# Gate pairs two to eight: the turning moved to VectorE, h added by accumulating loads, the finish of a pair moved behind the next pair

## The chip, the cores and the metric

The kernel runs on one core of one Trainium2 chip. Its time is the device time in microseconds of one execution. The five engines that the text speaks of are TensorE (PE; its weight loads are listed apart as PEld), VectorE (DVE), ScalarE (ACT), GpSimd (POOL) and SyncE (SP). SP issues most transfers; POOL issues the stores of the result.

## The reference

The reference is one inference step of a trunk with one layer, for T = 2080 rows (2048 of a prompt, 32 of a running stream) of width 1024, in float32. What matters here is the last of its three steps. With `h` the state after the mixers, `p` an input of 256 channels a row, and `g_final` a vector:

```
h   = h + concat(mixer_A, mixer_B) @ W_out
e   = p @ W_ple                                    # (T,256) @ (256,1024)
h   = h + e * sigmoid(rmsnorm(h) @ W_gate)         # (T,1024) @ (1024,1024)
out = rmsnorm(h) * g_final
```

The gate's product `rmsnorm(h) @ W_gate` has to be taken of the transposed rows, since TensorE contracts over partitions. The norm's factor is a number for each row; it is applied as the `scale` of the sigmoid.

## The kernel before

The 2080 rows are 16 tiles of 128 rows and a short one of 32. Every float32 operand of a product is split in two float32r parts: ACT copies it (L77, the high part), DVE subtracts that copy (L78, the low part), and three products (high·high, high·low, low·high) are added up in PSUM.

Products with square weights go by pairs of tiles: `seven` computes a pair's (256 x 1024) @ (1024 x 1024) product with seven half-size products in place of eight, each 12 matmuls of 128x128 by 128x512 (L167). The seven left operands are `11`, `12`, `22` and the sums `S1` to `S4`; the right ones are quarters of the weight and sums of them (`wg_a` to `wg_d`, `wg_T` and so on). A product lands in a PSUM bank (`x_g`, `y_g`, `z_g`), is carried (ACT copy) or is an output. `seven` takes a dictionary of steps to be recorded after its products, 1 to 6. A scheduler then orders the instructions of each engine; `tc.keep_in_program_order` pins one to its recorded place.

The stages of the program: input projection and mixers to about 560 us; the product with `W_out` by pairs to about 726 us; the embedding `e` in blocks (L102) to about 762 us, which writes `e` to DRAM, and meanwhile the gate's weights are loaded (`wg_r`, three buffers of the ring `xh`), split and added up on ACT and DVE; the short tile's gate (`gl`); eight gate pairs `g0` to `g14`, of about 20 us each; the last of them is `last_pair`, which computes the second tile's `e` itself (weights `wl`).

In a gate pair, while the products of pair `i` run, `prep_g(i + 2)` makes the left operands of the next one. The pair's second tile is loaded as four blocks (128 KB each) and turned by one DVE instruction (`turned_here`, STREAM_TRANSPOSE, L1293). The first tile is loaded as it is (`hn`, 512 KB), copied by ACT in two halves (`ho`, L1280) and turned by eight PE transposes into PSUM (`pth`, L1282). DVE makes the sums (L1426), and ACT and DVE split the results (L77, L78).

The outputs (`gate_ops`): ACT copies a bank (L1302), DVE adds a further product (L1310), ACT takes the sigmoid (L1308, L1311), DVE multiplies it into `e` (L1313) and adds that to `h` (L1314), for four halves a pair. `h` and `e` are loaded by SP. After the pair, for each of its tiles (`done_g`): squares on ACT (L88), mean and power on POOL (L69, L73), one DVE scaling by the root and `g_final` (SCALAR_TENSOR_TENSOR, L1321), and a store issued by POOL (L1322).

The buffers in question: `xh` has three (before: raw weights, then `h`), `ya` five (`hn`, `e`), `qa` two (`ho`), PSUM six banks for products and two for transposes.

Of the kernel before, what the change touches and what calls it, by code (L numbers as in the profile page):

```python
# [12 lines left out]
ALU = mybir.AluOpType  # L13
PSUM = bass.MemoryType.PSUM

P = 128
# [10 lines left out]
NT = SEQ // P + 1  # L27
NH = D // 2
# [6 lines left out]
def trunk(ctx, tc, x_p, x_s, c_conv, c_pool, p_p, p_s, g_mix, w_in, conv_w, conv_b, pool_w,  # L35
          pool_scale, w_out, g_ple, w_gate, w_ple, g_fin, y_p, y_s, sc_p, sp_p, sc_s, sp_s):
    nc = tc.nc
# [6 lines left out]
    h_d = tc.dram_tile([T, D], F32, name="h_d")  # L44
# [262 lines left out]
    def ring4(t, name):  # L307
        return t.tile([P, D], F32, tag="t", name=name)
# [15 lines left out]
    def load_rows(pool, name, i, pr, sa=None):  # L324
        r, n = tiles[i]
        t = ring4(pool, f"{name}_{i}")
        nc.sync.dma_start(t[:n], pr[r:r + n] if sa is None else rows_of(pr, sa, r, n))
        return t

    with ExitStack() as s1:  # L330
# [17 lines left out]
        def put(piece, src):  # L348

            split(piece[:, :, 0], piece[:, :, 1], src)  # L350
# [750 lines left out]
    with ExitStack() as s2:  # L1101
# [13 lines left out]
        def half_of(x, at, n=P):  # L1115
            return x[at[0]][:n, at[1] * NH:at[1] * NH + NH]
# [155 lines left out]
        def turned(i):  # L1272

            r, n = tiles[i]
            t = load_rows(ya, "hn", i, h_d).rearrange("p (q k c) -> p k q c", q=4, k=KC)
            out = []
            for half in range(2):
                pt = tbank(f"pth_{i}_{half}")
                o = qa.tile([P, KH, P], F32, tag="q", name=f"ho_{i}_{half}")
                nc.scalar.copy(o[:n].rearrange("p k (q c) -> p k q c", q=4), t[:n, half * KH:half * KH + KH])  # L1280
                for k in range(KH):
                    nc.tensor.transpose(pt[:, k * P:k * P + n], o[:n, k], ident[:n, :n])  # L1282
                out.append(pt.rearrange("p (k t) -> p k t", k=KH))
            return out

        def turned_here(i):

            r, n = tiles[i]
            t = ring4(ya, f"hn_{i}")
            for q in range(4):  # L1290
                nc.sync.dma_start(t[q * 32:q * 32 + 32].rearrange("p (g c) -> p g c", g=4),
                                  h_d[r:r + P, q * 256:q * 256 + 256].rearrange("(g p) c -> p g c", p=32))
            nc.vector.transpose(t, t)  # L1293
            u = t.rearrange("p (g k t) -> p k g t", g=4, k=KC)
            return u[:, :KH], u[:, KH:]

        def gate_ops(h, e, n, name, i):
            scale = lambda at: rs_h[:n, i + at[0]:i + at[0] + 1]

            def carry(ps, at):  # L1300
                t = st.tile([P, NH], F32, tag="t", name=f"c_{name}_{at[0]}{at[1]}")
                nc.scalar.copy(t[:n], ps[:n])  # L1302
                return t

            def out(ps, c, at):
                if c is None:
                    c = st.tile([P, NH], F32, tag="t", name=f"g_{name}_{at[0]}{at[1]}")
                    nc.scalar.activation(c[:n], ps[:n], AF.Sigmoid, scale=scale(at))  # L1308
                else:
                    nc.vector.tensor_tensor(c[:n], ps[:n], c[:n], op=ALU.add)  # L1310
                    nc.scalar.activation(c[:n], c[:n], AF.Sigmoid, scale=scale(at))  # L1311
                ee, hh = half_of(e, at, n), half_of(h, at, n)
                nc.vector.tensor_tensor(ee, ee, c[:n], op=ALU.mult)  # L1313
                nc.vector.tensor_tensor(hh, hh, ee, op=ALU.add)  # L1314

            return carry, out

        def done_g(i, h):
            r, n = tiles[i]
            rf = sumsq(h, n, f"f{i}")  # L1320
            nc.vector.scalar_tensor_tensor(h[:n], h[:n], rf[:n], g_bc[:n], op0=ALU.mult, op1=ALU.mult)  # L1321
            nc.gpsimd.dma_start(rows_of(y_p, y_s, r, n), h[:n])  # L1322

        def short_ops(h, e, n):
# [17 lines left out]
        def last_pair(i, A):  # L1342
# [72 lines left out]
        def prep_g(i):  # L1415

            A = {}
            whole = lambda t: t.rearrange("p k (g t) -> p k g t", g=4)

            def put(q, src, view=lambda t: t):  # L1420
                A[q] = cmb.tile([P, KH, 2, P], F32R, tag="c", name=f"g{i}_{q}")
                split(view(A[q][:, :, 0]), view(A[q][:, :, 1]), src)

            def comb(q, x, y, op, view=lambda t: t):
                t = ss.tile([P, KH, P], F32, tag="s", name=f"g{i}_f{q}")
                nc.vector.tensor_tensor(view(t), x, y, op=op)  # L1426
                return t

            lower = []

            def first():
                lower.extend(turned_here(i + 1))

            def second():
                a21, a22 = lower
                s1 = comb("S1", a21, a22, ALU.add, whole)
                a11, a12 = turned(i)
                put("11", a11)
                s2 = comb("S2", s1, a11, ALU.subtract)
                s3 = comb("S3", whole(a11), a21, ALU.subtract, whole)  # L1440
                put("12", a12)
                put("S2", s2)
                s4 = comb("S4", a12, s2, ALU.subtract)
# [17 lines left out]
        done_g(NT - 1, h)  # L1461
# [37 lines left out]
```

## Time and profile before

| | |
|---|---|
| median of three runs | 942.25 us (947.01, 942.25, 941.83) |
| profiled execution | 942.12 us, of which the span is 940.3 us |
| mean granted clock of TensorE | 0.994 |
| gate pairs two to seven | 19.93 to 20.15 us each |
| bytes moved | 127.23 MB read, 54.86 MB written |

The profile's page gives the busy time of each engine as a share of the span, the chain of work that ended last (followed back from the last instruction), groups of instructions with mean duration and what ended the idle time before them, and the transfers with their time to landing. Busy time of an engine beside the one that sets the end costs nothing.

### The profile page before, as it was taken

Reading aid. Unit: us, or ns where it says so; the run is one execution under the profiler, and the core shown is the slowest. Engines: PE = TensorE matmul, PEld = TensorE weight load, DVE = VectorE, ACT = ScalarE, POOL = GpSimd, SP = SyncE. Lnnn points to the kernel's source line nnn. Section 1 sums busy time; section 2 is a strip of 40 time slices with the busy share of each in tenths; the row PEclk is TensorE's granted clock in tenths of the full one; section 3 lists DMA queues with packets and bytes.
Section 4 is the critical chain, followed back from the end, with each engine's and each line's share of the span. In section 5 each row is a group of like instructions: output and inputs, shape, how many; then the busy total and the mean of one; then the engine's idle time right before and its main releaser. Section 6 shows DMA issues by size and latency. Waiting matters only on the chain.

```text
span 940.3 us, 13055 instructions
## 1 busy us (share of the span) xinstructions
PE 920.7 (98%) x4599; PEld 831.5 (88%) x4599; DVE 726.3 (77%) x1230; ACT 480.5 (51%) x890; POOL 126.2 (13%) x244
## 2 busy tenths in 40 slices
PE   7999999999999999999999999999999999999996
PEld 5999999999999999999999987888878868888885
DVE  6697998899587978785777588765554797888985
ACT  5554555454444554443454356334334875555564
POOL 2101222120000110000000010211211001211113
PEclk8999999999999999999999999999999999999999
DMA  8336586696952655418655359865785883566653
GB/s 247 101 105 172 143 243 197 182 255 207 423 166 80 178 161 144 151 52 287 198 167 176 117 176 305 263 194 170 217 253 171 307 274 130 201 227 209 216 207 112
DMA packets 133214, 182.96 MB, mean 195 GB/s; under 512 B 11164, under 2 KB 105116, under 8 KB 131869
## 3 DMA queue, kind: packets, MB, share of 16 engines
q1 hardware_dynamic: 117165, 131.70, 45.2%
q0 software_dynamic: 13248, 44.93, 14.9%
q10 hardware_dynamic: 2736, 5.51, 1.8%
q8 instruction: 36, 0.59, 0.3%
q14 instruction: 29, 0.24, 0.1%
HBM read 127.23 MB, written 54.86 MB: 194 GB/s over the span
## 4 chain that ended last, share of the span: by engine, by line
PE 74%; DMA 3%; DVE 2%; ACT 2%; issue 0%; POOL 0%; POOLq 0%; DVEq 0%; ACTq 0%
PE x_o L167 9%; PE x_g L167 9%; PE e L102 5%; PE z_g L167 5%; PE x_zab L556 5%; PE z_o L167 4%; PE x_ch L556 4%; PE x_zbv L556 4%; PE z_zab L556 2%; PE y_g L167 2%; PE y_o L167 2%; PE b L556 2%; PE v L556 2%; PE zb L556 2%; PE za L556 2%; PE c L556 2%
## 5 line engine op out<-in xcount | busy, mean ns | idle before, releaser
L77 ACT CAST y_S<-y_fS 128x512 fp32r<-128x512 f32 x32 | 19.5, 621 | 42.5 <-PE x_o L167 18.9
L102 PE MATMUL e<-wq,pps 128*128 128x512 f32 (+1 forms) x156 | 38.8, 399 | 0.2 <-ACT pps L77 0.2
L406 DVE SCALAR_TENSOR_TENSOR xt<-xt,rstd_x,g_bc 128x1024 f32<-128x1024 f32 (+2 forms) x18 | 23.1, 1282 | 19.4 <-POOL rstd_x L73 18.0
L167 PE MATMUL x_g<-wg_b,g_S 128*128 128x512 f32 x128 | 35.9, 390 | 0.0
L167 PE MATMUL x_o<-wo_b,y_S 128*128 128x512 f32 x128 | 35.8, 391 | 0.0
L556 PE MATMUL z_ch<-B,w_ch_S 128*128 128x416 f32 x168 | 34.3, 352 | 0.9 <-ACT U L851 0.9
L556 PE MATMUL z_zab<-B,w_zab_S 128*128 128x416 f32 x168 | 34.1, 351 | 0.5 <-ACT U L851 0.5
L556 PE MATMUL x_zab<-B,w_zab_S 128*128 128x416 f32 x168 | 34.5, 352 | 0.1
L556 PE MATMUL z_zbv<-B,w_zbv_S 128*128 128x416 f32 x168 | 34.2, 352 | 0.0
L556 PE MATMUL x_zbv<-B,w_zbv_S 128*128 128x416 f32 x168 | 34.1, 351 | 0.0
L556 PE MATMUL x_ch<-B,w_ch_S 128*128 128x416 f32 x168 | 34.0, 351 | 0.0
L102 PEld LDWEIGHTS e<-wq,pps 128*128 128x128 f32 (+1 forms) x156 | 27.4, 182 | 6.9 <-ACT pps L77 0.5
L556 PEld LDWEIGHTS z_ch<-B,w_ch_S 128*128 128x128 f32 x168 | 31.2, 188 | 1.6 <-ACT U L851 1.2
L556 PEld LDWEIGHTS z_zab<-B,w_zab_S 128*128 128x128 f32 x168 | 31.3, 188 | 1.1 <-ACT U L851 0.8
L556 PEld LDWEIGHTS x_zab<-B,w_zab_S 128*128 128x128 f32 x168 | 31.2, 188 | 1.0 <-DVE w_zab_S L78 0.4
L556 PEld LDWEIGHTS x_ch<-B,w_ch_S 128*128 128x128 f32 x168 | 31.4, 188 | 0.3
L556 PEld LDWEIGHTS x_zbv<-B,w_zbv_S 128*128 128x128 f32 x168 | 31.3, 188 | 0.3
L556 PEld LDWEIGHTS z_zbv<-B,w_zbv_S 128*128 128x128 f32 x168 | 31.3, 188 | 0.4
L69 POOL TENSOR_SCALAR ms_f<-ssq_f 128x1 f32<-128x1 f32 (+1 forms) x15 | 8.8, 585 | 160.7 <-ACT junk L88 160.7
L77 ACT CAST y<-y 128x512 fp32r<-128x512 f32 x24 | 14.8, 618 | 29.4 <-PE x_o L167 13.8
L1321 DVE SCALAR_TENSOR_TENSOR h<-h,rstd_f,g_bc 128x1024 f32<-128x1024 f32 (+1 forms) x15 | 19.3, 1284 | 12.7 <-POOL rstd_f L73 12.7
L167 PEld LDWEIGHTS x_o<-wo_b,y_S 128*128 128x128 f32 x128 | 24.0, 188 | 5.0 <-ACT c_o L1125 0.3
(570 smaller groups left out, 2670.7 us busy)
## 6 DMA issues: line engine op xcount, KB each, us to landing
y<-y_d SPq DMA_DIRECT2D x16, 512.0 KB, 12.7
x<-in_x_prompt_dram SPq DMA_DIRECT2D x16, 512.0 KB, 9.7
h_d<-x SPq DMA_DIRECT2D x16, 512.0 KB, 4.5
h<-h_d SPq DMA_DIRECT2D x16, 512.0 KB, 3.6
xt<-in_x_prompt_dram SPq DMA_DIRECT2D x15, 512.0 KB, 12.7
e<-e_d SPq DMA_DIRECT2D x15, 512.0 KB, 5.9
out_dram<-h POOLq DMA_DIRECT2D x14, 512.0 KB, 3.0
p_dT<-T POOLq DMA_DIRECT2D x12, 512.0 KB, 6.2
```

The source lines that it names most:

```text
L69: nc.gpsimd.tensor_scalar(ms[:n], ssq[:n], scalar1=1.0 / D, scalar2=EPS, op0=ALU.mult, op1=ALU.add)
L77: ins = nc.scalar.copy(hi, src)
L102: nc.tensor.matmul(ps[:n], pps[:, a, k, :n], wp[k][b][:, cs], start=k + q == 0, stop=k == 1 and q == 2)
L167: nc.tensor.matmul(ps[:n], lhs[:, k, a, :n], w[b][:, k], start=start and k + q == 0, stop=k == KH - 1 and q == 2, skip_group_check=True)
L406: nc.vector.scalar_tensor_tensor(xt[:n], xt[:n], r[:n], g_bc[:n], op0=ALU.mult, op1=ALU.mult)
L556: nc.tensor.matmul(ps[:, :NB], lhs[:, k, x], b[:, k, y], start=start and k + q == 0, stop=stop and k == KH - 1 and q == 2, skip_group_chec ...
L1321: nc.vector.scalar_tensor_tensor(h[:n], h[:n], rf[:n], g_bc[:n], op0=ALU.mult, op1=ALU.mult)
```

## The change

Four edits, all in the gate's pairs:

- `prep_g` has an argument `here`. For pairs two to eight (`here=True`) both tiles are loaded as four blocks each, at the start of the pair before, into the ring `xh`, and both are turned by DVE. For the first pair (`here=False`) the first tile is still turned by PE. All views of the operands are the blocks' (`whole`).
- `gate_ops` with `h is None` (all pairs but the last): the DVE addition of `h` goes; an accumulating load of the half tile of `h`, issued by POOL, adds it to the product of `e` and the sigmoid in place. The pair's tiles of `h` are not loaded any more, and the result stands in the buffer of `e`.
- `done_g` is cut in two, `root_g` (squares, mean, power) and `done_g` (scaling, store), both recorded in the next pair, at its steps 4 and 6; in `last_pair` at 4 and, behind the second half's last product, at 5.
- The scaling is pinned in program order (`keep_in_program_order`), and so are the squares (`later=True` of `sumsq`).

```diff
-        def turned_here(i):
+        def blocks(i):
             r, n = tiles[i]
-            t = ring4(ya, f"hn_{i}")
+            t = ring4(xh, f"hn_{i}")
             for q in range(4):
                 nc.sync.dma_start(t[q * 32:q * 32 + 32].rearrange("p (g c) -> p g c", g=4),
                                   h_d[r:r + P, q * 256:q * 256 + 256].rearrange("(g p) c -> p g c", p=32))
+            return t
+
+        def turned_here(t):
             nc.vector.transpose(t, t)
...
-                ee, hh = half_of(e, at, n), half_of(h, at, n)
+                ee = half_of(e, at, n)
                 nc.vector.tensor_tensor(ee, ee, c[:n], op=ALU.mult)
-                nc.vector.tensor_tensor(hh, hh, ee, op=ALU.add)
+                if h is None:
+                    r = tiles[i + at[0]][0]
+                    nc.gpsimd.dma_start(ee, h_d[r:r + P, at[1] * NH:at[1] * NH + NH], accum_op=ALU.add)
+                else:
+                    hh = half_of(h, at, n)
+                    nc.vector.tensor_tensor(hh, hh, ee, op=ALU.add)
...
-        def done_g(i, h):
+        def root_g(i, h, later=True):
+            return sumsq(h, tiles[i][1], f"f{i}", later=later)
+
+        def done_g(i, h, rf, later=True):
             r, n = tiles[i]
-            rf = sumsq(h, n, f"f{i}")
-            nc.vector.scalar_tensor_tensor(h[:n], h[:n], rf[:n], g_bc[:n], op0=ALU.mult, op1=ALU.mult)
+            ins = nc.vector.scalar_tensor_tensor(h[:n], h[:n], rf[:n], g_bc[:n], op0=ALU.mult, op1=ALU.mult)
+            if later:
+                tc.keep_in_program_order(ins)
             nc.gpsimd.dma_start(rows_of(y_p, y_s, r, n), h[:n])
...
-            seven(f"g{i}", A, W, carry, out, {5: lambda: second(1, NH)}, first_tile=True)
+            seven(f"g{i}", A, W, carry, out, {4: roots, 5: lambda: (second(1, NH), finished())}, first_tile=True)
...
-            lower = []
+            rows = [blocks(i + b) for b in range(1 - here, 2)]
+            ready = []
             def first():
-                lower.extend(turned_here(i + 1))
+                ready.extend(turned_here(rows[0]))
             def second():
-                a21, a22 = lower
-                s1 = comb("S1", a21, a22, ALU.add, whole)
-                a11, a12 = turned(i)
-                put("11", a11)
-                s2 = comb("S2", s1, a11, ALU.subtract)
+                if here:
+                    a11, a12 = ready
+                    put("11", a11, whole)
+                    a21, a22 = turned_here(rows[1])
+                    s1 = comb("S1", a21, a22, ALU.add, whole)
+                else:
+                    a21, a22 = ready
+                    s1 = comb("S1", a21, a22, ALU.add, whole)
+                    a11, a12 = map(whole, turned(i))
+                    put("11", a11, whole)
+                s2 = comb("S2", whole(s1), a11, ALU.subtract, whole)
...
-        for step in prep_g(0).values():
+        for step in prep_g(0, here=False).values():
...
+        def roots():
+            for x in ready:
+                x.append(root_g(*x))
+        def finished():
+            while ready:
+                done_g(*ready.pop(0))
         for i in range(0, NT - 3, 2):
             A = S.pop(i)
-            h = [load_rows(xh, "h", i + b, h_d) for b in range(2)]
+            steps = prep_g(i + 2)
             e = [load_rows(ya, "e", i + b, e_d) for b in range(2)]
-            seven(f"g{i}", A, W, *gate_ops(h, e, P, f"g{i}", i), prep_g(i + 2))
-            for b in range(2):
-                done_g(i + b, h[b])
+            seven(f"g{i}", A, W, *gate_ops(None, e, P, f"g{i}", i), {**steps, 4: roots, 6: finished})
+            ready.extend([i + b, e[b]] for b in range(2))
```

More of the change, by code (lines that the diff above doesn't have):

```diff
@@ L1411, in last_pair, with prep_g @@
             pps = embedded()
-            seven(f"g{i}", A, W, carry, out, {5: lambda: second(1, NH)}, first_tile=True)
+            seven(f"g{i}", A, W, carry, out, {4: roots, 5: lambda: (second(1, NH), finished())}, first_tile=True)
             second(0, NH // 2)
-        def prep_g(i):
+        def prep_g(i, here=True):
             A = {}
@@ L1427, in comb @@
                 return t
-            lower = []
+            rows = [blocks(i + b) for b in range(1 - here, 2)]
+            ready = []
             def first():
-                lower.extend(turned_here(i + 1))
+                ready.extend(turned_here(rows[0]))
             def second():
-                a21, a22 = lower
-                s1 = comb("S1", a21, a22, ALU.add, whole)
-                a11, a12 = turned(i)
-                put("11", a11)
-                s2 = comb("S2", s1, a11, ALU.subtract)
-                s3 = comb("S3", whole(a11), a21, ALU.subtract, whole)
-                put("12", a12)
+                if here:
[9 more added lines that the diff above has]
+                s2 = comb("S2", whole(s1), a11, ALU.subtract, whole)
+                s3 = comb("S3", a11, a21, ALU.subtract, whole)
+                put("12", a12, whole)
                 put("S2", s2)
-                s4 = comb("S4", a12, s2, ALU.subtract)
+                s4 = comb("S4", a12, whole(s2), ALU.subtract, whole)
                 put("S1", s1)
@@ L1460, in trunk @@
         plain("gl", A, W, n, *short_ops(h, e, n))
-        done_g(NT - 1, h)
+        done_g(NT - 1, h, root_g(NT - 1, h, False), False)
+        ready = []
+        def roots():
[4 more added lines that the diff above has]
+                done_g(*ready.pop(0))
         for i in range(0, NT - 3, 2):
             A = S.pop(i)
-            h = [load_rows(xh, "h", i + b, h_d) for b in range(2)]
+            steps = prep_g(i + 2)
             e = [load_rows(ya, "e", i + b, e_d) for b in range(2)]
-            seven(f"g{i}", A, W, *gate_ops(h, e, P, f"g{i}", i), prep_g(i + 2))
-            for b in range(2):
-                done_g(i + b, h[b])
+            seven(f"g{i}", A, W, *gate_ops(None, e, P, f"g{i}", i), {**steps, 4: roots, 6: finished})
+            ready.extend([i + b, e[b]] for b in range(2))
         last_pair(NT - 3, S[NT - 3])
```

## The prediction

> **What bounds the kernel now.** I read the page first: the shares of the engines, then the chain that ended last.
>
> ```profile
> PE 920.7 (98%) x4599; PEld 831.5 (88%) x4599; DVE 726.3 (77%) x1230; ACT 480.5 (51%) x890; POOL 126.2 (13%) x244
> PE 74%; DMA 3%; DVE 2%; ACT 2%; issue 0%; POOL 0%; POOLq 0%; DVEq 0%; ACTq 0%
> ```
>
> TensorE (PE) is busy 98% of the span and carries the chain; nothing else has more than 3% of it. The change concerns the last fifth, so next comes the table by windows there, one row per gate pair (columns: length, then PE, PEld, DVE, ACT and POOL busy, granted clock, share of the DMA engines, GB/s).
>
> ```profile
> 787.80:807.75 19.95, 19.95 (x93) 16.57 (x93) 17.65 (x27) 11.70 (x21) 3.49 (x6) 1.00 0.43 143
> 827.73:847.67 19.94, 19.94 (x94) 16.60 (x93) 17.43 (x27) 11.39 (x20) 3.36 (x6) 1.00 0.63 216
> 887.54:907.69 20.15, 20.15 (x95) 16.76 (x95) 17.67 (x27) 11.49 (x21) 3.36 (x6) 1.00 0.66 236
> 907.69:940.30 32.61, 24.61 (x109) 19.82 (x107) 22.30 (x36) 16.40 (x31) 10.40 (x16) 0.95 0.33 119
> ```
>
> A pair is 19.94 us of PE without a gap at full clock, so within a pair only PE work counts, as long as the others keep inside it. VectorE (DVE) is close behind with 17.4. Only in the last window is PE idle, for 32.61 − 24.61 = 8.0 us. The chain, read by start and duration, shows what PE does in a pair:
>
> ```profile
> 785.78 0.87 PE pth L1282 x8
> 786.65 1.15 PE z_g L167 x5
> 787.80 5.44 PE x_g L167 x24
> 793.24 2.72 PE y_g L167 x12
> 805.26 0.44 PE pth L1282 x4
> 805.93 0.44 PE pth L1282 x4
> ```
>
> Seven products of 12 matmuls at 2.72 are 19.04; the eight transposes (pth) are the other 0.87 to 0.88.
>
> **1. The transposes.** Pairs two to eight lose theirs: 56 of them, 7 × 0.88 = 6.2 us, all on the path.
>
> ```profile
> L1282 PE MATMUL pth<-ident,ho 128*128 128x128 f32 x56 | 7.4, 272 | 0.0
> L1280 ACT COPY ho<-hn 128x512 f32<-128x512 f32 x12 | 6.8, 622 | 0.0
> L1293 DVE STREAM_TRANSPOSE hn<-hn 128x1024 f32<-128x1024 f32 x6 | 7.4, 1237 | 0.0
> L1314 DVE TENSOR_TENSOR h<-h,e 128x512 f32<-128x512 f32 x24 | 15.9, 685 | 0.2
> ```
>
> The 7.4 counts overlapping ends, so it is the upper bound; I take 6.2, the chain's figure. In their place comes, per pair, one more STREAM_TRANSPOSE (1.24 on DVE), four adds of h go (4 × 0.685 = 2.74), and ScalarE (ACT) loses two copies (1.24). DVE in a pair: 17.43 + 1.24 − 2.74 = 15.9 of a new pair of 19.05; ACT: 11.39 − 1.24 = 10.1. The combinations then read SBUF where they read PSUM; rows of both kinds last the same (683 ns and 689 ns), so this costs nothing.
>
> ```profile
> L1426 DVE TENSOR_TENSOR g_fS<-pth,hn 128x512 f32<-128x512 f32 x7 | 4.8, 683 | 0.0
> L1426 DVE TENSOR_TENSOR g_fS<-hn 128x512 f32<-128x512 f32 x6 | 4.1, 689 | 0.2
> ```
>
> The Trainium skill ("VectorE: DVE Perf Modes", the table of rules for kernel authors) speaks against the change: a 128x128 transpose belongs on TensorE, since VectorE turns 32x32 blocks alone. By the rule's reckoning of the instructions alone it should lose, 1.24 on DVE against 0.88 on PE; the rows above say that here PE is the engine without slack and DVE the one with some, and the block loads bring the blocks to their places, so the sum goes by PE.
>
> **2. The accumulating loads.** Per pair two loads of h (512 KB, SyncE's queue) become four accumulating loads of 256 KB issued by GpSimd (POOL), each behind a product with the sigmoid; the whole load of hn becomes four blocks, as its partner already is. Bytes stay the same.
>
> ```profile
> q1 hardware_dynamic: 1327, 3.27, 50.7%
> q0 software_dynamic: 288, 1.05, 13.3%
> out_dram<-h POOLq DMA_DIRECT2D x2, 512.0 KB, 3.0
> h<-h_d SPq DMA_DIRECT2D x2, 512.0 KB, 4.3
> e<-e_d SPq DMA_DIRECT2D x2, 512.0 KB, 5.9
> hn<-h_d SPq DMA_DIRECT2D x4, 128.0 KB, 2.5
> L1322 POOL DMA_DIRECT2D out_dram<-h x12 | 6.9, 574 | 6.3 <-DVE h L1321 6.3
> ```
>
> These rows (one pair) put 64% of 19.98 us, 12.8 us, on 4.32 MB, or 3.0 us a MB. No accumulating transfer is in this trace. If it costs k times a plain one, a pair's DMA is 12.8 + (k − 1) × 3.1 and fits into 19.05 up to k = 3. Bounds: k = 1 by the nearest row (h, 4.3 us to landing for twice the bytes), and k = 4, beyond which nothing here points. POOL issues four more at 0.574: 3.36 + 2.3 = 5.7 of 19.05. Who waits for them: the squares on ACT, now at step 4 of the next pair; a pair's last product comes some 2 us into the next pair and step 4 follows four products, 4 × 2.72 = 10.9, so about 8 us are there for the last load, against 3.0 to 4.3 in the rows. Cost taken: 0; if the cover is gone, ACT stands still ahead of the casts and copies PE needs, and PE stops 1 for 1.
>
> The Trainium skill ("Collectives: The Full Stack", the section on the bandwidth ceiling and the fold count) has an add in a transfer read two sources and run at half the rate. By it k = 2 and a pair's DMA is an estimated 15.9 us, which still fits; no run here shows it yet.
>
> **3. The finish of a pair, later.** Squares, the mean and the power, two scalings (STT) and two stores move behind step 4 and step 6 of the next pair; at the scaling DVE waited for POOL:
>
> ```profile
> L1321 DVE SCALAR_TENSOR_TENSOR h<-h,rstd_f,g_bc 128x1024 f32<-128x1024 f32 x12 | 15.4, 1285 | 10.0 <-POOL rstd_f L73 10.0
> ```
>
> Ten us over six pairs; they go, since the root is ready some 2 us before the pinned place. PE was fed through them, so they are worth 0. On SyncE's queue the second e load now waits for a store of two pairs before, and everything behind it with it; the store is freed by the pinned scaling some 1.5 us into the pair and takes 3.0, the load 5.9, so it lands at about +10; its first reader comes after five products, 5 × 2.72 = +13.6. Cover: some 4 us.
>
> **4. The front.** In the order of the built program pair one's transposes, which stay on PE, stand after 10 of the 24 matmuls of the last embedding block (the second half after 11), no longer inside the short tile. Their operand is copied by ACT, and these copies (ho) stand behind the casts of the last gate weights, thus behind the last load of raw weights. Rows before (SyncE, DVE, ACT, PE):
>
> ```profile
> 754.37 0.32 SPq L1268 DMA_DIRECT2D wg_r<-g_d  x1
> 753.66 0.69 DVE L78 TENSOR_TENSOR wg_b<-wg_r,wg_b 128x512 fp32r<-128x512 f32 x1
> 758.53 0.62 ACT L77 CAST wg_c<-wg_r 128x512 fp32r<-128x512 f32 x1 [0.82 <-DMA wg_r<-g_d]
> 759.05 0.61 ACT L77 CAST wg_d<-wg_r 128x512 fp32r<-128x512 f32 x1
> 756.52 5.80 PE L102 MATMUL e<-wq,pps 128*128 128x512 f32 x24
> 763.87 1.14 ACT L1280 COPY ho<-hn 128x512 f32<-128x512 f32 x2
> 764.91 1.03 PE L1282 MATMUL pth<-ident,ho 128*128 128x128 f32 x8
> ```
>
> PE, with 5.80 / 24 = 0.24 a matmul, would reach the first half at 756.5 + 10 × 0.24 = 758.9. The wg loads stand earlier on SyncE's queue now, the fourth ahead of a store that it followed; I estimate that this brings the release of the last one's buffer, by the wg_b at 753.66, some 2.3 us forward, from 754.35 to 752. It then lands at 756.2 (as long as before, 758.53 − 754.37 = 4.2) to 757.25 (5.2, the stretch's usual). From there ACT has nine instructions before the first ho, which start 0.52 apart (759.05 − 758.53) or a little less, and two more to the second's end: 5.7 to 6.3 us, the longer where a cast waits for DVE. So the second half is ready at 761.9 (756.2 + 5.7) to 763.5 (757.25 + 6.3), while PE would reach it at 758.9 + 0.44 + 0.24 = 759.6. PE is held 2.3 to 3.9 us; I take 3.2, nearer to the usual landing. Bounds: 1.5 (a landing faster than the last) and 6 (as late as before). Where the load comes earlier still, 0.
>
> **5. The tail.** The last pair has no next pair, so pair seven's two pinned scalings stand behind step 5, just ahead of the last product's multiplication:
>
> ```profile
> 917.26 1.29 DVE L1321 SCALAR_TENSOR_TENSOR h<-h,rstd_f,g_bc 128x1024 f32<-128x1024 f32 x1 [0.73 <-POOL rstd_f L73]
> 921.05 1.28 DVE L1321 SCALAR_TENSOR_TENSOR h<-h,rstd_f,g_bc 128x1024 f32<-128x1024 f32 x1 [0.45 <-POOL rstd_f L73]
> 930.67 0.68 DVE L1372 TENSOR_TENSOR h<-h,c_g 128x512 f32<-128x512 f32 x1
> 932.77 0.75 DVE L1371 TENSOR_TENSOR g_l<-e_l,g_l 128x256 f32<-128x256 f32 x2 [1.42 <-ACT g_l L1401]
> ```
>
> Both now come between the last two rows, where DVE idles 1.42: 1.28 + 1.20 − 1.42 = +1.1 on the path to the end; I take 1.0. Their old places are waits for PE that stay. The weights wl now wait for pair six's pinned stores; I count about 1 us to spare, and below that 1 for 1.
>
> **Sum.** −6.2 + 3.2 + 1.0 = −2.0. The profiled execution took 942.12 (span 940.3), 0.13 below the median of 942.25; so 940.1 and, to the median, 940.3 us.
>
> **The rivals.** (a) *The front's cover holds*: ho ready before PE comes. For it, the loads stand earlier on the queue; against it, even the fastest load leaves ACT eleven instructions. −6.2 + 1.0 = −5.2: 937.0. (b) *The accumulating loads become the bound*, the slower side. For it: this transfer is in no row, and POOL's loads share the DMA engines, 0.63 busy. It decides from k = 3; at k = 4 a pair is 12.8 + 9.3 = 22.1, six pairs give 6 × 3.05 = +18.3, in all 958.6; from k = 3.4 it is slower by over 0.5%. The skill's k = 2 and the 4.3-us row speak against it. (c) *An in-order wait* in the steady pairs or the last: squares behind a late accumulation, the e load behind a late store, wl behind it. Cover 8, 4 and 1 us. If 1 us is lost in each of seven pairs, −2 + 7 = +5: 947. (d) *DVE becomes the bound*, so that the transposes' time isn't won: 15.9 of 19.05 with in-order waits of over 3 us a pair. Then the pairs stay at 19.95: +4.2, 946.5. The skill's rule on transposes would have it so; the sum of DVE's rows is against it.
>
> **How the numbers follow.** This kernel's measurement can tell about 0.5% (4.7 us) from no change: faster is below 937.5, slower above 947.0. Chances: the forecast 0.52 (938.5 to 942.5), (a) 0.17, (b) 0.09, (c) 0.13, (d) 0.09. Faster: (a) and a little, 0.19. Slower: (b), most of (c) and a part of (d), 0.21. Same: 0.60. The range goes from (a), 936.5, to the top of (c) and (d), 948; outside lie (b), the far part of (c), and a little under (a).
>
> **What would show it.** In the changed profile: pairs of 19.05 with PE busy throughout (1 right; 19.95 means (d), 22 means (b)); the accumulating loads' time to landing and the DMA share, 0.67 if k is 1 and 0.83 if k is 2 (2); no wait of the scaling for POOL (3); a hole in PE of 2.3 to 3.9 us between 759 and 764 ended by ACT's ho (4; none means (a)); two scalings right before the last multiplications (5). I am wrong if the pairs aren't 0.9 shorter, or a wait of several us stands where none is named above.

## The result: slower by 0.7%, and the profile after

| | before | after |
|---|---|---|
| median of six runs, us | 944.47 (941.83 to 947.01) | 951.04 (947.15 to 953.1) |
| ratio | | 1.0072 (95%: 1.0044 to 1.0099) |
| profiled execution, us (span) | 942.12 (940.3) | 951.98 (950.2) |

The prediction was 940.3 with a range of 936.5 to 948.0: the time lies outside, on the slow side. The change made each undisturbed pair as much shorter as was forecast, and lost more ahead of the pairs, behind them and in one of them.

To compare two traces stage by stage I use three marks of TensorE (PE): the first transposes of the short tile, the first y_g product of the first pair, and that of the last pair. "Front" lies between the first two, "pairs" (seven of them) between the last two, "tail" from the last to the end of the span. The rows of the timeline (start, duration, engine, what), before:

```profile
755.91 0.68 PE L1282 MATMUL pth<-ident,ho 32*128 32x32 f32 x8
773.14 0.39 PE L167 MATMUL y_g<-wg_c,g 128*128 128x512 f32 x1
913.00 0.39 PE L167 MATMUL y_g<-wg_c,g 128*128 128x512 f32 x1
```

and after:

```profile
758.57 0.43 PE L1282 MATMUL pth<-ident,ho 32*128 32x32 f32 x4
780.43 0.39 PE L167 MATMUL y_g<-wg_c,g 128*128 128x512 f32 x1
916.34 0.39 PE L167 MATMUL y_g<-wg_c,g 128*128 128x512 f32 x1
```

| stage, us | before | after | difference |
|---|---|---|---|
| to the first mark | 755.91 | 758.57 | +2.66 |
| front | 17.23 | 21.86 | +4.63 |
| pairs | 139.86 | 135.91 | −3.95 |
| tail | 27.30 | 33.86 | +6.56 |
| span | 940.3 | 950.2 | +9.9 |

Of the first 2.66 us, 2.64 are there at 540 us already, where both programs have the same instructions in the same order on every engine. They arise at one place, where PE waits for an operand that ACT splits (before, then after):

```profile
273.87 0.64 PE L704 MATMUL pm<-pp,pw 128*128 128x416 f32 x2 [1.55 <-ACT pp L77]
275.15 1.06 PE L704 MATMUL pm<-pp,pw 128*128 128x416 f32 x2 [3.19 <-ACT pp L77]
```

Behind the longer wait the granted clock falls as well. The same wait lasts from 1.55 to 3.19 us in the fourteen traces of this case, so this is the spread between executions; the change's own difference is 7.24, beside 6.57 between the medians.

**Pairs.** The windows after, as in the prediction's table:

```profile
797.00:816.00 19.00, 19.00 (x85) 15.75 (x84) 15.13 (x23) 10.05 (x18) 6.46 (x9) 1.00 0.83 176
835.00:856.10 21.10, 19.35 (x86) 15.71 (x85) 17.05 (x24) 10.63 (x18) 7.06 (x11) 1.00 0.87 220
913.30:950.20 36.90, 24.30 (x99) 18.73 (x97) 18.99 (x26) 13.82 (x27) 12.39 (x20) 0.87 0.47 147
```

Six of the pairs take 19.03 to 19.31, PE busy throughout, DVE 15 to 18 us; the fourth takes 21.07. The share of the DMA engines (next to last column) is 0.77 to 0.91 where it was 0.43 to 0.68. In the last window the clock is 0.87, and PE is idle for 12.6 us in place of 8.0. The table of waits, which had no row for PE over the gate's pairs before, names the three holes (total, times, longest, in us):

```profile
PE pth L1282 <- DVE pps L78: 2.9, 1, 2.9
PE x_g L167 <- ACT c_g L1306: 1.8, 1, 1.8
PE x_g L167 <- DVE c_g L1314: 1.7, 1, 1.7
```

**Front.** Rows of PE, SyncE and ACT after:

```profile
761.86 0.43 PE L1282 MATMUL pth<-ident,ho 32*128 32x32 f32 x4 [2.86 <-DVE pps L78]
762.22 4.09 PE L102 MATMUL e<-wq,pps 128*128 128x512 f32 x10
754.26 0.32 SPq L1268 DMA_DIRECT2D wg_r<-g_d  x1
760.33 0.62 ACT L77 CAST wg_c<-wg_r 128x512 fp32r<-128x512 f32 x1 [2.37 <-DMA wg_r<-g_d]
761.33 0.22 ACT L77 CAST pps<-ptp 128x64 fp32r<-128x64 f32 x1
```

PE stands 2.86 us ahead of the short tile's second transposes. They want one of the two PSUM banks for transposes, which is free when DVE has split the last embedding operand (pps); ACT's part of that split stands behind the cast that waits for the last raw weights, and these land 6.1 us after their issue. The ten matmuls behind the hole take 4.09 us in place of 2.4. The windows show why (the last three columns are the clock, the DMA share and GB/s):

```profile
758.60:762.00 3.40, 0.54 (x7) 0.43 (x7) 1.56 (x4) 1.67 (x5) 0.00 (x0) 1.00 0.29 106
762.00:764.00 2.00, 2.00 (x10) 1.58 (x10) 1.87 (x3) 2.00 (x5) 0.00 (x0) 0.72 0.85 294
764.00:766.50 2.50, 2.50 (x9) 1.91 (x8) 2.31 (x6) 2.50 (x7) 0.00 (x0) 0.54 0.90 311
```

In these 4.5 us behind the hole the granted clock is 0.72 and 0.54 in the mean, and that costs another 1.7 us (4.09 less 2.4). Together they are 4.55 of the 4.63.

**Tail.** The rows, in the order of the chain (SyncE, ACT, PE):

```profile
920.45 1.58 SPq L1239 DMA_DIRECT2D wlr<-in_w_ple_dram  x2
924.90 1.04 ACT L77 CAST wl<-wlr 128x1024 fp32r<-128x1024 f32 x1 [4.12 <-DMA wlr<-in_w_ple_dram]
926.49 1.90 PE L167 MATMUL x_g<-wg_b,g_S 128*128 128x512 f32 x4 [1.82 <-ACT c_g L1306]
928.53 3.76 PE L167 MATMUL z_g<-wg_d,g_S 128*128 128x512 f32 x12
```

The raw weights wl are issued only at 920.45, when the stores of pair six are through; ACT's cast waits for them, the copy that PE needs stands behind the cast, PE stops for 1.82 us, and then works at a lower clock (0.50 for 3.4 us; 12 matmuls took 2.96 before). From the y_g product to the S3 product that follows z_g it is 15.79 us in place of 11.87. Another 1.85 us are DVE's (DVE, then GpSimd):

```profile
938.48 3.48 DVE L1332 SCALAR_TENSOR_TENSOR e<-e,rstd_f,g_bc 128x1024 f32<-128x1024 f32 x2
941.88 0.74 DVE L1384 TENSOR_TENSOR g_l<-e_l,g_l 128x256 f32<-128x256 f32 x2
939.19 1.69 POOL L1391 TENSOR_TENSOR hg<-h,g_bc 128x512 f32<-128x512 f32 x1
```

The two pinned scalings take 3.48 us beside GpSimd's product, against 2.48 for two in the pairs. The last 0.8 lie behind the last multiplication: the last store ends 4.5 us after its issue, 3.7 before.

**Transfers.** Over 797 to 914 us after (queue: packets, MB, share; then issues, KB each, us to landing), and in the last row the blocks over the six pairs before:

```profile
q0 software_dynamic: 5080, 11.88, 45.9%
e<-h_d POOLq DMA_DIRECT2D x26, 256.0 KB, 5.7
e<-e_d SPq DMA_DIRECT2D x12, 512.0 KB, 7.1
hn<-h_d SPq DMA_DIRECT2D x44, 128.0 KB, 4.9
out_dram<-e POOLq DMA_DIRECT2D x10, 512.0 KB, 5.0
hn<-h_d SPq DMA_DIRECT2D x24, 128.0 KB, 2.8
```

An accumulating load of 256 KB takes 5.7 us, and everything beside it has become slower: blocks 4.9 for 2.8, stores 5.0 for 3.0, e loads 7.1 for 5.9. Experiment 4 shows how much of this is the accumulating.

### The profile page after: what moved, and what is told of

Its sections match the earlier page's. It is cut to its first block, busy times and chain, and to the rows that moved or that the text cites. A ratio compares the mean times of both kernels' runs of the same rounds, so it can differ in the third digit from the quotient of the medians.

```text
span 950.2 us, 13005 instructions
## 1 busy us (share of the span) xinstructions
PE 919.0 (97%) x4543; PEld 827.3 (87%) x4543; DVE 719.2 (76%) x1209; ACT 473.3 (50%) x876; POOL 146.9 (15%) x272
## 5 line engine op out<-in xcount | busy, mean ns | idle before, releaser
L102 PE MATMUL e<-wq,pps 128*128 128x512 f32 (+1 forms) x156 | 40.9, 412 | 0.2 <-ACT pps L77 0.2
L1320 POOL DMA_DIRECT2D e<-h_d x28 | 24.7, 903 | 56.9 <-DVE e L1317 45.0
L167 PEld LDWEIGHTS x_g<-wg_b,g_S 128*128 128x128 f32 x128 | 24.3, 190 | 7.3 <-ACT c_g L1306 2.2
```

Of the source, the lines that this page charges most:

```text
L102: nc.tensor.matmul(ps[:n], pps[:, a, k, :n], wp[k][b][:, cs], start=k + q == 0, stop=k == 1 and q == 2)
L167: nc.tensor.matmul(ps[:n], lhs[:, k, a, :n], w[b][:, k], start=start and k + q == 0, stop=k == KH - 1 and q == 2, skip_group_check=True)
L1320: nc.gpsimd.dma_start(ee, h_d[r:r + P, at[1] * NH:at[1] * NH + NH], accum_op=ALU.add)
```

## The experiments

All stage times are taken by the three marks above, from one profiled execution of each kernel. "Before" beside a median is the kernel before, run on the same chip beside it, and the ratio is that of the two. The changed kernel's own ratio is 1.0072.

| | median (before), us | ratio | front | pairs | tail |
|---|---|---|---|---|---|
| 1 front as before | 945.85 (942.65) | 1.0033 | 17.23 | 134.50 | 34.66 |
| 2 wl in the other ring | 948.29 (942.65) | 1.0070 | 23.04 | 135.62 | 30.08 |
| 3 scalings first | 952.40 (942.65) | 1.0108 | 22.14 | 138.09 | 35.36 |
| 4 plain loads | 946.59 (942.65) | 1.0042 | 22.88 | 133.84 | 31.65 |
| 5 mended | 942.00 (943.00) | 0.9985 | 17.23 | 136.79 | 29.49 |
| 6 PE turns again | 954.22 (943.00) | 1.0112 | 22.56 | 140.12 | 36.97 |
| 7 accumulated twice | 1017.83 (943.00) | 1.0800 | 22.68 | 186.07 | 50.11 |
| 8 queue order pinned | 942.55 (942.23) | 1.0004 | 17.44 | 137.71 | 29.62 |
| 9 turning alone | 939.93 (942.23) | 0.9975 | 17.23 | 136.75 | 28.20 |
| 10 half the accumulations | 949.75 (942.23) | 1.0086 | 17.27 | 142.56 | 32.22 |
| 11 turning, one sum on GpSimd | 942.39 (942.42) | 1.0004 | 17.24 | 138.48 | 28.52 |
| 12 mended, plain loads | 939.21 (942.42) | 0.9963 | 17.24 | 134.67 | 29.49 |

### 1. The front's order

```diff
-            rows = [blocks(i + b) for b in range(1 - here, 2)]
+            rows = [blocks(i + b, xh if here else ya) for b in range(1 - here, 2)]
```

> The first pair's blocks go into the ring of five again, as before the change; everything else is the changed kernel. PE and ACT then stand in the front in the order of the kernel before. Theory (the front loses by order: the cast of the last embedding operand, for whose PSUM bank the short tile's second transposes wait, stands behind the cast that waits for the last raw weights): no hole in PE at the short tile's transposes, and from those transposes to the first y_g product 17.2 us as before, in place of 21.9 in the changed kernel; the whole 4 to 5 us shorter than the changed kernel's 951.0. Rival (the front loses because the last raw load lands late, 6.1 us after its issue against 4.2 before): the hole of some 3 us moves elsewhere in the front and it stays at 20 us or more. Tail 33.9 by both.

The front is 17.23 us, to the hundredth as before, without a hole, and the ratio falls from 1.0072 to 1.0033, some 3.7 us. So the front's whole loss comes from one buffer: the first pair's blocks in the ring of three changed the order that the scheduler gave ACT, and with it the orders of PE and of SyncE's queue. The run gives all three back together and does not separate them. The tail kept its loss.

### 2. The ring of wl

```diff
-            wp = embedding_chunks("wl")
+            wp = embedding_chunks("wl", xh)
```

> The last pair's raw weights wl are loaded into the ring of three that the blocks have left, so that they no longer wait for the stores of pair six; the rest is the changed kernel. Theory (the tail loses 1.8 us in a PE stall behind ACT's cast of wl, and 2 more by the lower clock that follows): the stall goes, the twelve z_g matmuls behind it take 2.9 us in place of 3.8, and the stretch from the last pair's first y_g to the end falls from 33.9 to 29.5 to 30.5, the rest being the two scalings. Rival (accumulating transfers make all transfers late there): wl still lands late and PE waits 1 us or more.

The tail's stall is gone, and with it the lower clock:

```profile
922.50:926.30 3.80, 3.80 (x18) 2.98 (x17) 0.00 (x0) 2.79 (x5) 1.69 (x6) 1.00 0.05 8
```

The tail is 30.08, 3.8 us shorter, as the theory said. The rival falls: nothing was changed in the accumulating loads. In the whole time, though, this mend alone does not show: the ratio is 1.0070 (1.0046 to 1.0093), as the changed kernel's, and the profiled execution is the second fastest of ten, with a front 1.2 us longer. The stall's part rests on this one trace, and on experiment 5.

### 3. The scalings ahead of the last product

```diff
-            ... 5: lambda: (second(1, NH), finished())}, first_tile=True)
+            ... 5: lambda: (finished(), second(1, NH))}, first_tile=True)
```

> In the last pair the two pinned scalings of pair seven are recorded ahead of the second half's last product, no longer behind it; the rest is the changed kernel. Theory (the two scalings, 3.5 us on DVE ahead of the last products' multiplication, cost 2 us of the tail): the last multiplication comes 1.2 to 2 us sooner after PE's end, the tail falls from 33.9 to 32 to 32.6. Rival (the tail is set by the final stores or by the stall alone): within 0.5 us of 33.9. By either the stall of 1.8 us behind the wl cast stays.

A miss. From the addition that follows z_g to the last store's issue it is 13.35 us, in the changed kernel 13.37: the two scalings, at 1.28 each now, stood in another place of the same line of DVE work. The stalls were 1.6 and 0.8, and behind them the clock went to 0.50:

```profile
930.40:935.70 5.30, 5.30 (x13) 4.14 (x14) 1.28 (x1) 2.14 (x4) 1.77 (x5) 0.50 0.00 0
```

### 4. Plain loads in place of the accumulating ones

```diff
-                    nc.gpsimd.dma_start(ee, h_d[...], accum_op=ALU.add)
+                    nc.gpsimd.dma_start(ee, h_d[...])
```

> The 28 accumulating loads become plain loads of the same halves of h by the same queue at the same places, so h replaces the product in the buffer and no sum is made (this part of the computation is left out); the instruction order of all engines is the changed kernel's. Theory (accumulating costs about twice a plain load, but in the pairs is hidden; tail and front lose by order): the time to landing falls from 5.7 us to about 3.5, the queue's share of the DMA engines from 46% to about 30%, the single stall of 1.75 us in the pairs may go; tail and front stay within 1.5 us of 33.9 and 21.9. Rival (accumulation is the common cause, through full DMA engines): the tail falls by 3 us or more, as wl lands in time.

The same window as above, here:

```profile
q0 software_dynamic: 3520, 12.06, 32.2%
e<-h_d POOLq DMA_DIRECT2D x26, 256.0 KB, 4.2
hn<-h_d SPq DMA_DIRECT2D x44, 128.0 KB, 3.7
out_dram<-e POOLq DMA_DIRECT2D x12, 512.0 KB, 4.4
e<-e_d SPq DMA_DIRECT2D x12, 512.0 KB, 6.4
```

The queue's share falls by 13.7% of 117 us, 16.0 us over 26 loads or 6.8 MB: accumulating costs 2.35 us a MB over the plain 3.12 (0.322 × 117 / 12.06), a factor of 1.75. The other transfers land sooner as well: blocks in 3.7, stores in 4.4, e loads in 6.4. So of their delay (2.1, 2.0 and 1.2 us) some half is the accumulating, 1.2, 0.6 and 0.7; the rest is there with plain loads too. The pairs' stall goes (133.84). Tail and front: 31.65 and 22.88; the tail fell by 2.2, more than the theory's 1.5 and less than the rival's 3. Accumulation is a part of the tail's loss, and nothing of the front's: without it ACT casts wl 6.97 us after the tail's mark instead of 8.56, PE's holes are 0.24 and 0.98, and behind them the clock stays at 1.00.

### 5. Three mends together

Experiments 1 and 2, and:

```diff
-            ... {4: roots, 5: lambda: (second(1, NH), finished())}, first_tile=True)
+            ... {4: lambda: (roots(), finished()), 5: lambda: second(1, NH)}, first_tile=True)
```

> Three mends on the changed kernel: the first pair's blocks in the ring of five (as in the first experiment), wl in the ring of three (as in the second), and in the last pair both the squares and the two scalings of pair seven recorded at step 4, ahead of the z_g product's output. Theory (front and tail lose by order, the accumulating loads cost little): front 17.2 us, pairs 134.5 to 135.6, tail 27.3 to 28.3; against the kernel before 0, -4.3 to -5.4 and 0 to +1, so 937.5 to 939.5 where before has 942.65. Rival (the accumulating loads cost as much as the transposes did): the tail stays above 29.5 or the pairs above 137, and it is no faster than before, 941 or more.

942.0 against 943.0, a ratio of 0.9985 (0.9969 to 1.0002): not told from before. The front is mended; the pairs (136.79, with two stalls) and the tail (29.49) lie between what the theory and the rival expected, and the whole is the rival's, 941 or more.

```profile
PE x_g L167 <- DVE c_g L1314: 1.3, 1, 1.3
PE z_g L167 <- ACT c_g L1306: 1.1, 1, 1.1
```

### 6. PE turns the first tiles again

```diff
-            steps = prep_g(i + 2)
+            steps = prep_g(i + 2, here=False)
...
-            t = load_rows(ya, "hn", i, h_d)...
+            t = load_rows(ya if i in (0, NT - 1) else xh, "hn", i, h_d)...
```

> The first tile of every pair is turned by PE again (8 transposes a pair, two copies on ACT); accumulating loads, later finish and pins are the changed kernel's, the whole load of hn goes into the ring of three. Theory (PE alone sets a pair's length, 0.88 us for eight transposes): pairs two to seven 19.92 to 19.97 where no wait falls, the stretch of seven pairs 139.9 to 142 in place of 135.9, the whole 5 to 6 us longer than the changed kernel: 956 to 957. Rival (with the accumulating loads a pair is set by waits for transfers, not by PE): the stretch within 2 us of the changed kernel's 135.9.

The pairs two to six are 19.93 to 19.94 each, as in the kernel before, and the seven take 140.12: PE alone sets a pair that has no stall, and eight transposes cost what the prediction said. The whole is 954.22, less than the 956 to 957 that were expected: the pairs are 4.2 us longer than the changed kernel's and not 6.2, since here they have no stall. The tail, which the expectation left out, is 3.1 longer, with holes of 2.93 and 0.97 in PE.

### 7. Each accumulation twice

```diff
                     nc.gpsimd.dma_start(ee, h_d[...], accum_op=ALU.add)
+                    nc.gpsimd.dma_start(ee, h_d[...], accum_op=ALU.add)
```

> Each accumulating load is issued twice, so h is added twice (the result is not the reference's); nothing else changes. In the changed kernel the DMA engines are 85% busy over the pairs, 46% with POOL's queue. Theory (an accumulated MB costs 1.75 times a plain one, 3.1 us, and the pairs are near but below the bound): 1.05 MB more a pair is 5.4 us more, 16.3 + 5.4 = 21.7 us of transfers in a pair of 19.05, so DMA becomes the bound: pairs of 21 to 23 us, the whole 15 to 30 us longer than the changed kernel. Rival (accumulation costs only time to landing, not share): the pairs stay at 19.05 to 20 us and the whole within 6 us.

A ratio of 1.08 to before (1.0775 to 1.0825), far past what was expected, and not for the reason under test. The second load of a half waits for the first one's landing, and GpSimd's queue stands meanwhile:

```profile
L1321 POOL DMA_DIRECT2D e<-h_d x28 | 24.3, 870 | 112.1 <-DMA e<-h_d 112.1
```

112 us of waits stand in that row. The DMA engines did not become the bound (81% busy over 797 to 914 us). This run says what an in-order wait on a DMA-issuing engine costs, and nothing on the price of a MB.

### 8. The order of SyncE's queue

```diff
+                if ring is None:
+                    tc.keep_in_program_order(ins)   # each block load of the pairs, and likewise each e load
```

> The mended kernel of the fifth experiment, with SyncE's block loads and e loads of the pairs pinned in the order in which they are written: a pair's eight blocks ahead of its two e loads, so that no block stands behind an e load of the same pair that waits for a store. Theory (the stalls in the pairs, 2.4 us there, come from blocks queued behind the e load, which makes the turn on DVE late): the seven pairs take 133.6 to 134.4 in place of 136.8, tail and front as in the mended kernel (29.5 and 17.2); 938.5 to 940.0 against 943.0 before. Rival (the accumulating loads make the transfers late in any order): a stall of 1 us or more stays in the pairs, which take 135.5 or more.

A miss: 137.71, with four stalls. The blocks stand ahead of their pair's e loads now, but behind those of the pair before:

```profile
844.52 13.44 SPq L327 DMA_DIRECT2D e<-e_d  x2
858.04 6.94 SPq L1293 DMA_DIRECT2D hn<-h_d  x8
```

The second of these two e loads waits until its buffer has been stored (such waits of the queue last up to 12.6 us here), and so the two take 13.44 us. The order alone doesn't free the queue.

### 9. The turning alone

The kernel before, with both tiles of pairs two to eight loaded as blocks and turned by DVE; h, its addition and the finish as before.

```diff
             def first():
-                lower.extend(turned_here(i + 1))
+                if here:
+                    upper.extend(turned_here(i))
+                else:
+                    lower.extend(turned_here(i + 1))
```

> The kernel before with one part of the change alone: in pairs two to eight both tiles are loaded as blocks (in the ring of five, as before) and turned by DVE. h is loaded by SyncE and added by DVE, and the finish follows its own pair, as before. Theory (without the other two parts DVE becomes the bound: 17.4 + 1.24 = 18.7 us of work and 1.7 of waits for POOL in a pair): pairs of 19.6 to 20.4 in place of 19.95, the whole within 3 us of before. Rival (PE alone sets the pair, DVE's waits overlap): pairs of 19.05, seven pairs 133.4, and 936 to 937.5.

939.93 against 942.23: a ratio of 0.9975 (0.9961 to 0.9989), and the only kernel here that leaves nothing out and is clear of the noise faster than both. The theory (19.6 to 20.4, within 3 us of before) fits the third to sixth pair, 19.62 to 19.65, though not the first two, 19.08 and 19.24; the rival's 19.05 is reached in none. PE has no wait over 0.3 us, and DVE is busy 92% of the time:

```profile
845.00:865.00 20.00, 19.96 (x88) 15.83 (x87) 18.36 (x26) 10.72 (x19) 4.27 (x6) 1.00 0.68 213
```

### 10. Half of the accumulations

```diff
+            h1 = load_rows(xh, "h", i + 1, h_d)
-            ... gate_ops(None, e, P, f"g{i}", i)
+            ... gate_ops([None, h1], e, P, f"g{i}", i, True)   # the second tile's sum on DVE
```

> The mended kernel with 14 accumulating loads in place of 28: h of each pair's second tile is loaded by SyncE into the ring of three and added by DVE. Theory (accumulation lengthens all transfers, and the pairs' stalls and half of the tail's loss come from it): landing of the loads below 5 us, stalls in the pairs 0 to 1 us, the stretch 133.6 to 135; the tail 28 to 29.5. Rival (the third buffer of the ring of three was what kept the blocks early): the blocks come later, the stretch takes 137 or more.

The number is the rival's, 142.56 with four holes in PE of 5.6 us, three of them in the pairs, ended by ACT's splits of the sums, though the accumulating loads land in 4.9 us. Its reason is not seen: DVE waits for no block in this run. The turns stand in DVE's line behind the two pinned scalings, without idle time before them, and sums of h stand among the operand's sums:

```profile
870.59 2.48 DVE L1333 SCALAR_TENSOR_TENSOR e<-e,rstd_f,g_bc 128x1024 f32<-128x1024 f32 x2
872.98 1.24 DVE L1297 STREAM_TRANSPOSE hn<-hn 128x1024 f32<-128x1024 f32 x1
```

So this run changed DVE's order along with the loads, and does not tell what half of the accumulating is worth.

### 11. One sum of four on GpSimd

The kernel of experiment 9, and:

```diff
-                nc.vector.tensor_tensor(hh, hh, ee, op=ALU.add)
+                (nc.gpsimd if at == (0, 0) and n == P else nc.vector).tensor_tensor(hh, hh, ee, op=ALU.add)
```

> The kernel of the ninth experiment (both tiles turned by DVE, nothing else), with one of the four additions of h in each pair moved from DVE to GpSimd. Theory (that kernel's pairs of 19.63 are set by DVE, 18.66 us of it busy, which makes the S2 split late by 0.1 to 0.2 us at a time): DVE loses 0.69 us a pair, the pairs fall to 19.05 to 19.3, the seven to 133.5 to 135, and the whole is 1.5 to 3 us shorter than the ninth's 939.9. Rival (GpSimd's addition slows DVE's instructions beside it, as the two scalings beside GpSimd's product in the tail: 3.48 in place of 2.47): pairs of 19.6 or more and no gain.

The rival again: pairs of 19.98, no gain. Over the pairs of this run (GpSimd, then DVE):

```profile
L1314 POOL TENSOR_TENSOR h<-h,e 128x512 f32<-128x512 f32 x6 | 9.9, 1654 | 18.7 <-DVE e L1313 18.7
L78 DVE TENSOR_TENSOR g<-hn,g 128x512 fp32r<-128x512 f32 x18 | 18.4, 1052 | 0.0
```

and the same splits in experiment 9:

```profile
L78 DVE TENSOR_TENSOR g<-hn,g 128x512 fp32r<-128x512 f32 x18 | 11.8, 683 | 0.0
```

Six additions that DVE would do in 0.69 take GpSimd 1.65 each, and 18 of DVE's splits go from 683 to 1052 ns in the mean: in each pair the two that run beside the addition take 2.38 us together, and the others stay at 0.69 each. DVE loses 6.6 us and gains 4.1.

### 12. The mended kernel with plain loads

Experiment 5, and:

```diff
-                    nc.gpsimd.dma_start(ee, h_d[...], accum_op=ALU.add)
+                    nc.gpsimd.dma_start(ee, h_d[...])
```

> The mended kernel of the fifth experiment with plain loads in place of the accumulating ones (h replaces the product, so the sum is left out); the order of all engines' instructions is the fifth's. Theory (what the mended kernel still lacks, 136.8 in place of 133.4 in the pairs and 29.5 in place of 27.3 in the tail, is the price of accumulating): pairs 133.4 to 134.2, tail 27.5 to 28.7, 937 to 939 against the fifth's 942.0. Rival (the queue's order holds the blocks whatever the loads cost): a stall of 1 us or more stays, pairs 135.5 or more.

Here too the sum is left out. 939.21 and a ratio of 0.9963 against the fifth's 942.0 and 0.9985, the pairs 134.67 with one stall of 0.7, just above the theory's 134.2; so some 2.1 us of the fifth's pairs are the price of accumulating. The tail is 29.49 in both: the 2.2 us that it lacks are not that price.

## Why the prediction was wrong, step by step

**Step 1, the transposes, held.** Undisturbed pairs take 19.03 to 19.05 for 19.94 before, and PE's turning put back gives 19.93 (experiment 6). The Trainium skill's rule that a 128x128 transpose belongs on TensorE ("VectorE: DVE Perf Modes", the table of rules) would have had the change lose here; experiment 9, the turning alone, gains 0.25%. But DVE is then 93% busy (111.97 of 120 us), and the pairs stop at 19.63 instead of 19.05: rival (d) is two thirds true for the turning without the other parts. That DVE causes those 0.6 us is what the profile suggests and no run shows; experiment 11, meant to show it, ran into another price.

**Step 2, "cost taken: 0", failed.** The price of a MB was inside its bounds (k = 1 to 4) at 1.75, and DMA stayed below the bound at 0.77 to 0.91 of a pair; rival (b) was rightly small. That bytes stay the same did not keep the share at the 0.67 of k = 1, though: with plain loads the two queues are busy 40.6% and 32.2% of the window, 0.73 (experiment 4). By the rule of the Trainium skill ("Collectives: The Full Stack", the bandwidth ceiling and the fold count) an add in the path halves the rate, k = 2; the measured 1.75 is near it. What I left out is who shares the engines. I gave the cover of the loads' own readers (8 us, and ACT's squares indeed waited only 1.1 us), and none for the blocks, the e loads and the stores, each 1.2 to 2.1 us later (0.6 to 1.2 of it by accumulating, experiment 4), nor for wl behind the stores. Experiments 4 and 12 put the price at some 2.1 us in the pairs, and experiment 4 at 2.2 in the changed kernel's tail. It is not a fixed price: in experiments 1 to 3, which leave the accumulating loads as they are, the stall in the pairs is 0.64, 1.47 and 2.35 us, and the last of them brings the clock down as well (134.50, 135.62 and 138.09).

**Step 3, "cover: 4 us", failed.** It was counted for the e load. I had written that everything behind it waits with it, and did not price the blocks there. In the fourth pair after, which begins at 837.82 (SyncE, DVE, PE):

```profile
843.00 0.34 SPq L327 DMA_DIRECT2D e<-e_d  x1
843.39 5.71 SPq L1291 DMA_DIRECT2D hn<-h_d  x7
851.45 1.25 DVE L1297 STREAM_TRANSPOSE hn<-hn 128x1024 f32<-128x1024 f32 x1 [3.58 <-DMA hn<-h_d]
853.32 3.01 PE L167 MATMUL x_g<-wg_T,g 128*128 128x512 f32 x12 [1.75 <-DVE c_g L1314]
```

The first three of these blocks are the turn's, behind the e load, which had waited 8.0 us for a store. The turn waits 3.58 us for the last of them, and the addition that frees PE's bank stands behind it on DVE. It is rival (c), in one pair of seven. With plain loads (experiment 4) the same e load is issued 3.45 us into the pair instead of 5.18, the turn starts at 11.25 instead of 13.63, and PE doesn't wait: most of the delay comes by the late store. Experiment 8 shows that the order of the queue alone isn't its cure, and 4 that plain loads are.

**Step 4, the front, was right in kind, wrong in place and a third too small.** 4.63 for 3.2. The buffer's release, 752 by my estimate, is 751.6 when the 2.66 us of the two executions are taken off. The load took 6.1 us where I had 4.2 to 5.2. The hole stands ahead of the short tile's transposes, one place earlier than I looked: I followed the operand (ho) and overlooked the bank. And it is 2.86 us, inside my 2.3 to 3.9; the other 1.7 us are the lower clock behind it, a term that the sum did not have.

**Step 5, the tail, failed most: 6.56 for 1.0.** The 1 us that I counted as spare for wl was too much: the first store of pair six was issued at 914.50 and wl could follow at 920.45, 6 us where I had 3.0 for the store; that used the spare up and 1.82 more (experiment 2). The lower clock behind that made it 3.9. The store's 3.0 was wrong without the accumulating too: with plain loads (experiment 4) wl follows 5.6 us behind the store's issue, but is there 3.2 us later and not 4.5. The scalings, 2.48 by their row less 1.42 of idle time, took 3.48 beside GpSimd's product, which I had not looked for.

**The sum again,** with what was measured: −6.2 (transposes), +2.2 (stall and small delays in the pairs), +4.6 (front), +6.6 (tail) gives +7.2; between the medians it is 6.6. The mended kernel has the front back and 4.4 of the tail, and its ratio to before includes 1.

What stays open: the last 2.2 us of the mended tail. Its rows show two half additions of h that take 1.55 us together, 0.75 before, beside GpSimd's product, and a last store that ends 4.5 us after its issue for 3.7 before; the other 0.6 lie ahead of the last multiplication. No run separates them.

## What to carry to other kernels

Where work is taken off the engine that sets the pace, look at the borders of the loop first: the saved 0.88 us a pair came out as forecast, while one buffer moved to another ring cost five of them through the order that the scheduler then chose. For every load that waits longer, list what is queued behind it, on its own queue and, once it lands, on the engine that consumes it in order. When one part of a change carries the gain, run that part alone: the turning without the accumulating loads was better (a ratio of 0.9975) than the whole change (1.0072).

## What the runs showed of the hardware

A short hole in PE can cost as much again in clock. Behind holes of 2.86, 1.82 and 1.6 + 0.8 us (front and tail after, tail of experiment 3) the matmuls took longer: twelve of them 3.76 us (tail after) and 5.49 us (experiment 3) for 2.96; behind the hole of 1.75 us in the fourth pair the clock stayed. Where the clock falls it is halved for 3.4 us, which costs 1.7 us if PE has work throughout (front and tail after):

```profile
762.88:766.26 3.38, 3.38 (x10) 2.50 (x9) 3.38 (x7) 3.38 (x9) 0.00 (x0) 0.50 0.90 303
926.80:930.14 3.34, 3.19 (x8) 1.98 (x7) 2.21 (x2) 3.26 (x7) 1.97 (x4) 0.50 0.00 0
```

In the front of experiment 4 and the tail of experiment 3 it stays halved for twice as long, 6.8 us. Over the fourteen traces, from 25 us on, no hole of 0.9 to 1.78 us by itself brought the clock down; seven of ten between 1.80 and 2.55 us did, and every one of 2.60 us and more. The length alone does not decide: at the same place of the program, near 273 us, a hole of 1.80 us did (experiment 8) and one of 2.55 us did not (experiment 10). The Trainium skill ("TensorE: Matmul & The Clock Gate", "What's actually happening") has a free-running window of about 3.4 us, after an idle one of which the clock halves; the 3.4 us, the half clock and the part that a hole's place plays agree with these traces, but the clock fell here after holes well under 3.4 us.

An accumulating load (float32, 256 KB, DRAM to SBUF) takes 1.75 times the DMA share of a plain one and 0.90 us of GpSimd to issue, for 0.56 (experiment 4).

A GpSimd instruction that reads SBUF slows some DVE instructions beside it: two scalings 3.48 us for 2.48, two splits 2.38 us (experiment 11) where two take 1.29 without it (experiment 9). The Trainium skill ("SBUF — State Buffer", "Who interferes with whom") names a port pair that the two share, for DVE instructions with two SBUF inputs; the trace agrees.
